# One core, decoder layer: a new deal of filler products, four banks of branch B begun early, three w_up low parts on GpSimd

## The chip, the cores and the metric

The kernel runs on 1 core of one Trainium2 chip. The metric is the device time of one execution in microseconds (us). The kernel before takes 712.83 us as the median of 3 runs (712.62 to 714.18).

## What is computed

One layer on x of 512 tokens x 1024 features, float32. Cut to what matters here:

```python
h = rms_norm(x, g_mix)
z = h @ w_in                     # q,k,v of branch A | q,k,v of branch B | gate logits
ya = swa_sink_attention(qa, ka, va, sinks, bias_a)      # window 128, 8 query heads, blocks of 128
ob = diff_attention(qb, kb, vb, lam, bias_b)            # (softmax1 - lam softmax2) V, 4 heads, causal
yb = rms_norm(ob, subln_b)
mixed = sigmoid(gA) * (ya @ w_br_a) + sigmoid(gB) * (yb @ w_br_b)
x = x + mixed @ w_o
u = causal_dwconv3(rms_norm(x, g_ffn) @ w_up)           # 1024 -> 2 x 2816
x = x + (silu(u_gate) * u_value) @ w_down
```

## The kernel before

**Products.** Every float32 factor is split into a high part (rounded by a copy) and a low part (what is left), and a product is three matmuls: high by high, high by low, low by high (`mm3`, L171 to L174). A step of 128 features against 512 tokens is three matmuls of 128x512.

**Weights.** They come in units of 128x1024, in the fixed order `worder`. `split_unit` (L125) loads a unit into `raw` on SyncE's queue, makes the high part on ScalarE (L131) and the low part on VectorE or, for the units in the set `pooled` (L158), on GpSimd (L132). `raw`, high and low have three buffers each, and `wunit` asks for one unit ahead (AHEAD = 1). So a unit's high part waits until TensorE is done with the unit three before it.

**Order of the work.** TensorE's instructions run in the order in which the code is written; those of the other engines are put in order by a scheduler when the kernel is built. Attention has many short steps that wait for VectorE and ScalarE, so between them the code calls `fill(name, i)`: it takes so many steps as the table `FILL` says out of a stream `fs` of long products that nothing waits for (gate banks, branch A's product, projections of branch B, and at the end `br_b_early`). A filler step is one `mm3`, or four for each k of a projection taken one at a time. When the stream is empty, a fill does nothing.

**Branch A (sliding window).** `fill("q")`, the heads' transposes, `fill("k")`, the key's parts (`k_parts`; high on ScalarE L463 and L465, low on VectorE L467), `fill("k2")`, and then eight units. Round i does the score of unit i (L471, L472), the transposes of unit i-1 (L626) and the product of unit i-2 (L643, L645), with the fills s1, s2, s3 behind them.

**Branch B (differential).** Sixteen units, four heads by four query blocks; unit u is head u // 4, block u % 4. Round i does:

- score i (L471, L472), then fill a[i]. Behind it on VectorE maxima (L704 where there are far keys, L706), the negative maximum (L709), on ScalarE the exponentials (L711), on VectorE the reciprocals (L714, L715), ScalarE's scaling (L716) and VectorE's difference (L717);
- the product of unit i-2 (`diff_av`: L743 with the high part, L746 with the low; then ScalarE L749, VectorE L750, ScalarE L751), then fill c;
- the transposes of unit i-1 (L727; high part on ScalarE L728, low on VectorE L729), then fill b;
- in the rounds that `r` names, a head's RMS norm (`diff_rms`: short operations on 128x4, L181 to L190 and L207, then L759 on VectorE and L761 on ScalarE) and fill d; in the rounds that `o` names, a head's transposes into yb (`diff_out`: L767; high part ScalarE L768, low VectorE L769) and fill e.

`f` are fills behind the key and query parts of heads 2 and 3; p0 to p2 stand ahead of the first unit.

**End of branch B.** Once head 2 is out, `br_b_early` joins the stream: it begins EARLY banks of yb @ w_br_b with their first three steps (heads 0 to 2). After head 3, the early banks get their fourth step, first the two matmuls that need only the high part (L878), then the third (L882); the other banks (8 - EARLY) are made in full. `mix` behind each bank (L868, L869 on VectorE; the split on ScalarE L871 and GpSimd L872) makes the left side of W_o. `late` starts two banks of W_o with steps 0 to 5 of both, then steps 6 and 7.

**w_up.** 44 banks, each with a `conv` behind it: L956 on VectorE scales by the tokens' row `rbc`, which is ready only after the fourth bank; L959 and L969 are ScalarE's, L963, L964 and L971 VectorE's. w_down follows as seven products of halves.

Of the kernel before, what the change touches and what calls it, by code (L numbers as in the profile page):

```python
# [65 lines left out]

FILL = dict(r=[5, 9, 13, 16], o=[6, 10, 14, 16], e=[5, 1, 1, 40], kv=4, up=3, warm=8, q=7, k=19, k2=4,
            s1=[0, 3, 0, 3, 2, 4, 4, 0, 0, 3], s2=[2, 3, 0, 5, 1, 7, 5, 5, 0, 0],  # L70
            s3=[3, 0, 2, 5, 6, 2, 2, 6, 0, 1], p0=4, p1=3, p2=10, ud=6, pd=[8, 9], f=[9, 0],
            a=[6, 1, 7, 8, 10, 2, 0, 5, 0, 2, 7, 3, 6, 0, 0, 5],
            b=[6, 2, 4, 4, 2, 7, 2, 1, 2, 2, 0, 0, 1, 4, 2, 2], c=[3, 0, 0, 0, 2, 0, 0, 0, 2, 1, 0, 0, 1, 0, 0, 0],
            d=[1, 0, 0, 5], v0=4)
AHEAD = 1
EARLY = 5


@with_exitstack
def tile_decoder_layer(ctx: ExitStack, tc: tile.TileContext, x4, wall, cst_d, relb_d, oneh_d, xn_d, out):  # L80
# [1091 lines left out]
```

## Time and profile before

| what | value |
|---|---|
| median of 3 runs | 712.83 us (712.62 to 714.18) |
| the profiled execution | 711.81 us |
| its span, first to last instruction | 710.0 us |
| mean granted TensorE clock | 0.995 |
| VectorE busy | 486.1 us |
| ScalarE busy | 371.3 us |
| GpSimd busy | 196.8 us |
| low parts on VectorE | 102, mean 1226 ns |
| low parts on GpSimd | 33, mean 2411 ns |

The profile is of one execution. Rows of the timeline read: start, duration, engine, line, operation, what is written and read, the tile's form, the count, and in brackets the idle time of the engine before it and who ended it. A matmul row's duration is modelled and overlaps the next; the start-to-start time of two rows is what a matmul costs. "PEld" is the load of a matmul's weights. In the rows of a table by windows stand the window, its length, then busy time and count of TensorE, weight load, VectorE, ScalarE and GpSimd, the granted clock, the share of DMA and GB/s.

### The profile page before, as it was taken

The page shows a single profiled execution, that of the slowest core. Times are in us where ns is not written, and L with a number is a line of the kernel's source. Part 1 is how long each engine was busy: PE and PEld are TensorE (multiplying, and loading weights), DVE is VectorE, ACT ScalarE, POOL GpSimd, SP SyncE. Part 2 cuts the span into 40 slices and gives each one's busy share as a digit, 9 for nine tenths or more (in the row PEclk, how much of TensorE's full clock was granted, in tenths as well). Part 3 has the DMA queues.
Part 4 walks back from the last instruction along what each step waited for, and adds up shares of the span by engine and source line. Part 5 has one row for each costly group of instructions (what it writes and reads, how often), then busy time and mean ns, then how long its engine had stood idle before and what let it go on. Part 6 is the DMA issues. An engine that isn't in the chain of part 4 may idle for free.

```text
span 710.0 us, 9146 instructions
## 1 busy us (share of the span) xinstructions
PE 690.0 (97%) x3220; PEld 568.2 (80%) x3220; DVE 486.1 (68%) x978; ACT 371.3 (52%) x690; POOL 196.8 (28%) x168
## 2 busy tenths in 40 slices
PE   7999999999999989989999999999999999999997
PEld 5897888778888867768888788888888888888886
DVE  5686786567517787585438868777767677788783
ACT  5537777865336867434325344343334334766661
POOL 2144254533347310283300514332123120100000
PEclk9999999999999999999999999999999999999999
DMA  8672112112232211035422896997986432566773
GB/s 306 260 267 90 60 60 90 59 60 90 70 109 69 80 60 61 30 108 163 144 90 79 281 297 190 324 292 196 266 237 158 138 107 87 162 192 188 228 219 107
DMA packets 28493, 107.86 MB, mean 152 GB/s; under 512 B 3652, under 2 KB 3936, under 8 KB 27936
## 3 DMA queue, kind: packets, MB, share of 16 engines
q1 hardware_dynamic: 21568, 73.67, 31.0%
q0 software_dynamic: 4816, 18.92, 11.9%
q10 hardware_dynamic: 2064, 14.70, 5.5%
q8 instruction: 25, 0.41, 0.2%
q14 instruction: 20, 0.16, 0.1%
HBM read 105.16 MB, written 29.64 MB: 190 GB/s over the span
## 4 chain that ended last, share of the span: by engine, by line
PE 87%; DVE 5%; ACT 5%; issue 1%; DMA 1%; SPq 0%; ACTq 0%; DVEq 0%
PE pj L174 22%; PE pj L172 22%; PE pj L173 22%; PE at L173 5%; PE at L174 5%; PE at L172 5%; DVE g L869 1%; PE at L472 1%; PE at L471 1%; DMA g<-in_x_dram 1%; DVE wlo L132 1%; PE at L626 1%; ACT p L711 1%; DVE g L868 1%; PE at L442 1%
## 5 line engine op out<-in xcount | busy, mean ns | idle before, releaser
L131 ACT ACTIVATE whi<-raw 128x1024 fp32r<-128x1024 f32 x135 | 139.4, 1035 | 152.7 <-PE pj L173 99.1
L172 PE MATMUL pj<-xg,whi 128*128 128x512 f32 x480 | 189.5, 395 | 0.0
L174 PE MATMUL pj<-xg,wlo 128*128 128x512 f32 x480 | 187.7, 391 | 1.2 <-DVE wlo L132 1.2
L173 PE MATMUL pj<-xg,whi 128*128 128x512 f32 x480 | 187.6, 391 | 0.0
L132 DVE TENSOR_TENSOR wlo<-raw,whi 128x1024 fp32r<-128x1024 f32 x102 | 124.8, 1226 | 35.5 <-ACT whi L131 35.0
L132 POOL TENSOR_TENSOR wlo<-raw,whi 128x1024 fp32r<-128x1024 f32 x33 | 79.4, 2411 | 113.8 <-ACT whi L131 108.2
L174 PEld LDWEIGHTS pj<-xg,wlo 128*128 128x128 f32 x480 | 90.4, 188 | 20.6 <-DVE wlo L132 1.7
L172 PEld LDWEIGHTS pj<-xg,whi 128*128 128x128 f32 x480 | 90.5, 189 | 18.1 <-ACT whi L131 0.4
L173 PEld LDWEIGHTS pj<-xg,whi 128*128 128x128 f32 x480 | 90.4, 188 | 17.9
L172 PE MATMUL pj<-whi,xg 128*128 128x512 f32 (+1 forms) x156 | 59.2, 379 | 1.8 <-ACT xg L286 1.8
L956 DVE TENSOR_TENSOR u<-pj,rbc 128x512 f32<-128x512 f32 x44 | 30.2, 689 | 42.2 <-PE pj L174 42.1
L174 PE MATMUL pj<-whi,xg 128*128 128x512 f32 (+1 forms) x156 | 58.3, 374 | 0.1
L173 PE MATMUL pj<-wlo,xg 128*128 128x512 f32 (+1 forms) x156 | 58.0, 372 | 0.0
L172 PE MATMUL at<-whi,xg 128*128 128x512 f32 x146 | 57.3, 393 | 0.0
L174 PE MATMUL at<-whi,xg 128*128 128x512 f32 x146 | 57.0, 390 | 0.0
L173 PE MATMUL at<-wlo,xg 128*128 128x512 f32 x146 | 56.9, 390 | 0.0
L959 ACT ACTIVATE yc<-u,cst 128x512 f32<-128x512 f32 x44 | 35.3, 806 | 9.4 <-DVE u L956 9.1
L963 DVE SCALAR_TENSOR_TENSOR yc<-u,cst,yc 128x511 f32<-128x511 f32 x44 | 35.6, 810 | 2.9 <-ACT yc L959 2.9
L969 ACT ACTIVATE yc<-yc 128x512 f32<-128x512 f32 x22 | 13.9, 632 | 44.6 <-DVE yc L964 44.2
L172 PEld LDWEIGHTS pj<-whi,xg 128*128 128x128 f32 x156 | 29.9, 192 | 7.0 <-ACT xg L286 2.2
L964 DVE SCALAR_TENSOR_TENSOR yc<-u,cst,yc 128x510 f32<-128x510 f32 x44 | 34.1, 777 | 1.3
L174 PEld LDWEIGHTS pj<-whi,xg 128*128 128x128 f32 x156 | 29.8, 191 | 5.7 <-DVE xg L287 0.5
(251 smaller groups left out, 1152.0 us busy)
## 6 DMA issues: line engine op xcount, KB each, us to landing
raw<-in_w_dram SPq DMA_DIRECT2D x108, 512.0 KB, 3.4
tsum<-in_w_dram POOLq DMA_DIRECT2D x24, 512.0 KB, 11.8
raw<-tsum SPq DMA_DIRECT2D x20, 512.0 KB, 3.7
tsum<-in_w_dram ACTq DMA_DIRECT2D x12, 512.0 KB, 6.9
tsum<-tsum ACTq DMA_DIRECT2D x12, 512.0 KB, 6.4
scr<-scr POOLq DMA_DIRECT2D x1, 2304.0 KB, 11.3
xnat<-in_xn_dram SPq DMA_DIRECT2D x2, 1024.0 KB, 9.4
tmp<-in_x_dram POOLq DMA_DIRECT2D x8, 256.0 KB, 3.3
```

Source lines behind the costliest of these rows:

```text
L131: nc.scalar.activation(hi[:, :width], raw[:, :width], AF.Copy)
L132: eng.tensor_tensor(lo[:, :width], raw[:, :width], hi[:, :width].bitcast(F32), ALU.subtract)
L172: nc.tensor.matmul(ps, a[0], b[0], start=start, stop=False, skip_group_check=skip)
L173: nc.tensor.matmul(ps, a[0], b[1], start=False, stop=False, skip_group_check=skip)
L174: nc.tensor.matmul(ps, a[1], b[0], start=False, stop=stop, skip_group_check=skip)
L442: nc.tensor.transpose(ps[:, t * P:(t + 1) * P], zs[t][:, c0:c0 + P], ident)
L471: nc.tensor.matmul(ps, q[:, qsl], kh[:, ksl], start=True, stop=False)
L956: nc.vector.tensor_tensor(u, ps, rbc2, ALU.mult)
L959: i = nc.scalar.activation(y, u, AF.Identity, bias=cst[:, C_CB + ch:C_CB + ch + 1], scale=cw[2])
L963: nc.vector.scalar_tensor_tensor(y[:, 1:S], u[:, 0:S - 1], cw[1], y[:, 1:S], ALU.mult, ALU.add)
L964: nc.vector.scalar_tensor_tensor(y[:, 2:S], u[:, 0:S - 2], cw[0], y[:, 2:S], ALU.mult, ALU.add)
L969: nc.scalar.activation(yg, yg, AF.Silu)
```

## The change

Three things, with no change to what is computed and none to the number of TensorE's matmuls.

1. `FILL` is dealt out anew: fewer or more filler steps at many places, head 1's output two rounds later (o from 10 to 12), head 3's norm named 17 instead of 16, which is the same round.
2. EARLY is 4 instead of 5: three filler steps fewer in the stream, and one full bank more behind head 3.
3. `pooled` also holds units 4 to 6 of w_up: their low parts move from VectorE to GpSimd.

```diff
-FILL = dict(r=[5, 9, 13, 16], o=[6, 10, 14, 16], e=[5, 1, 1, 40], kv=4, up=3, warm=8, q=7, k=19, k2=4,
-            s1=[0, 3, 0, 3, 2, 4, 4, 0, 0, 3], s2=[2, 3, 0, 5, 1, 7, 5, 5, 0, 0],
...
+FILL = dict(r=[5, 9, 13, 17], o=[6, 12, 14, 17], e=[5, 0, 2, 40], kv=4, up=3, warm=8, q=7, k=17, k2=7,
+            s1=[2, 0, 0, 3, 2, 2, 3, 0, 11, 3], s2=[0, 4, 0, 4, 1, 1, 5, 5, 2, 0],
...
-EARLY = 5
+EARLY = 4
...
-    pooled = {u + i for u, n in ((U_DA, 4), (U_VB, 4), (U_DB, 4), (U_BRA, 4), (U_GATE, 16), (U_BRB + 3, 1)) for i in range(n)}
+    pooled = {u + i for u, n in ((U_DA, 4), (U_VB, 4), (U_DB, 4), (U_BRA, 4), (U_GATE, 16), (U_BRB + 3, 1), (U_UP + 4, 3)) for i in range(n)}
```

**TensorE at score 11.** Before, head 1's output (L767) stands ahead of score 11 (L471, L472), which reads keys `qv`; `pj` is a gate bank, a filler.

```order
L172 MATMUL pj_2707<-xg_182,whi_2608 128x512
L173 MATMUL pj_2707<-xg_183,whi_2608 128x512
L174 MATMUL pj_2707<-xg_182,wlo_2609 128x512
L767 MATMUL at_2744<-ident,o_2301 128x128 x4
L172 MATMUL pj_2707<-xg_193,whi_2608 128x512
L173 MATMUL pj_2707<-xg_194,whi_2608 128x512
L174 MATMUL pj_2707<-xg_193,wlo_2609 128x512
L471 MATMUL at_2757<-qv_2466,qv_2453 128x512
L472 MATMUL at_2757<-qv_2464,qv_2453 128x512
L471 MATMUL at_2763<-qv_2467,qv_2454 128x512
L472 MATMUL at_2763<-qv_2465,qv_2454 128x512
```

Now the same gate bank ends behind score 11, and the product of unit 9 (L743) follows at once:

```order
L472 MATMUL at_2750<-qv_2456,qv_2445 128x512
L172 MATMUL pj_2707<-xg_182,whi_2608 128x512
L173 MATMUL pj_2707<-xg_183,whi_2608 128x512
L174 MATMUL pj_2707<-xg_182,wlo_2609 128x512
L172 MATMUL pj_2707<-xg_193,whi_2608 128x512
L173 MATMUL pj_2707<-xg_194,whi_2608 128x512
L174 MATMUL pj_2707<-xg_193,wlo_2609 128x512
L743 MATMUL at_2771<-vb_1834,ath_2731 128x256
L743 MATMUL at_2771<-vb_1837,ath_2731 128x256
L746 MATMUL at_2771<-vb_1834,atl_2732 128x128
L746 MATMUL at_2771<-vb_1837,atl_2732 128x128
```

Head 1's output has gone from here to behind unit 11's transposes, and unit 9's product stands three filler steps earlier behind score 11 than it did (before, three more steps of the next gate bank lay between).

**VectorE at units 14 and 15.** `p_2943` is unit 14's before, `p_3007` unit 15's. Before, unit 14's difference (L717) follows the low part of a weight of branch B and comes ahead of unit 15's maxima:

```order
L132 TENSOR_TENSOR wlo_3076<-raw_3073,whi_3075 128x1024
L717 SCALAR_TENSOR_TENSOR p_2943<-p_2943,drc_2962 128x384
L769 SCALAR_TENSOR_TENSOR y_2354<-at_2997,gsub,y_2353 128x512
L704 ISA p_3007,m_630_3013<-at_3010,cst 128x256
L704 ISA m_630_3013 128x1
L704 ISA p_3007,m_632_3019<-at_3016,cst 128x256
L704 ISA m_632_3019 128x1
L706 ISA p_3007,dmx_3008<-at_3010,bias_b,m_630_3013 128x256
L706 ISA dmx_3008 128x1
L706 ISA p_3007,dmx_3008<-at_3016,bias_b,m_632_3019 128x256
L706 ISA dmx_3008 128x1
L709 TENSOR_SCALAR dnmx_3022<-dmx_3008 128x2
```

Now unit 14's tile is `p_2961`, with `drc_2980`:

```order
L704 ISA p_3007,m_632_3019<-at_3016,cst 128x256
L704 ISA m_632_3019 128x1
L714 RECIPROCAL drc_2980<-dsm_2963 128x2
L706 ISA p_3007,dmx_3008<-at_3010,bias_b,m_630_3013 128x256
L706 ISA dmx_3008 128x1
L715 TENSOR_TENSOR drc_2980<-drc_2980,neglam 128x1
L706 ISA p_3007,dmx_3008<-at_3016,bias_b,m_632_3019 128x256
L706 ISA dmx_3008 128x1
L132 TENSOR_TENSOR wlo_3095<-raw_3092,whi_3094 128x1024
L717 SCALAR_TENSOR_TENSOR p_2961<-p_2961,drc_2980 128x384
L709 TENSOR_SCALAR dnmx_3022<-dmx_3008 128x2
```

The order of unit 14's L717 and unit 15's maxima is turned round: L769 and unit 15's four operations, and the low part, all come first, and unit 15's L709 has gone behind L717.

**VectorE in w_up.** `u_3970` is the bank c = 7 after L956, `wlo_3942` the low part for c = 8, `wlo_3993` for c = 9. Before:

```order
L956 TENSOR_TENSOR u_3970<-pj_3945,rbc_3620 128x512
L132 TENSOR_TENSOR wlo_3942<-raw_3939,whi_3941 128x1024
L963 SCALAR_TENSOR_TENSOR yc_3972<-u_3970,cst,yc_3972 128x511
L964 SCALAR_TENSOR_TENSOR yc_3972<-u_3970,cst,yc_3972 128x510
L971 TENSOR_TENSOR g_3979<-yc_3933,yc_3972 128x512
L132 TENSOR_TENSOR wlo_3993<-raw_3990,whi_3992 128x1024
L956 TENSOR_TENSOR u_4021<-pj_3996,rbc_3620 128x512
```

Now:

```order
L956 TENSOR_TENSOR u_3970<-pj_3945,rbc_3620 128x512
L963 SCALAR_TENSOR_TENSOR yc_3972<-u_3970,cst,yc_3972 128x511
L964 SCALAR_TENSOR_TENSOR yc_3972<-u_3970,cst,yc_3972 128x510
L971 TENSOR_TENSOR g_3979<-yc_3933,yc_3972 128x512
L956 TENSOR_TENSOR u_4021<-pj_3996,rbc_3620 128x512
L132 TENSOR_TENSOR wlo_3993<-raw_3990,whi_3992 128x1024
L132 TENSOR_TENSOR wlo_4032<-raw_4029,whi_4031 128x1024
```

The low part for c = 8 now stands two banks earlier (behind the L956 of c = 5), and that for c = 9 has gone behind the L956 of c = 8.

More of the change, by code (lines that the diff above doesn't have):

```diff
@@ L65 @@
 F_ORDER = [f + NH * j for f in range(NH) for j in range(2)]
-FILL = dict(r=[5, 9, 13, 16], o=[6, 10, 14, 16], e=[5, 1, 1, 40], kv=4, up=3, warm=8, q=7, k=19, k2=4,
-            s1=[0, 3, 0, 3, 2, 4, 4, 0, 0, 3], s2=[2, 3, 0, 5, 1, 7, 5, 5, 0, 0],
[L71 to L74, printed above, removed]
+FILL = dict(r=[5, 9, 13, 17], o=[6, 12, 14, 17], e=[5, 0, 2, 40], kv=4, up=3, warm=8, q=7, k=17, k2=7,
+            s1=[2, 0, 0, 3, 2, 2, 3, 0, 11, 3], s2=[0, 4, 0, 4, 1, 1, 5, 5, 2, 0],
+            s3=[5, 1, 2, 4, 8, 3, 6, 6, 0, 1], p0=4, p1=1, p2=10, ud=6, pd=[8, 9], f=[11, 0],
+            a=[6, 1, 6, 8, 10, 2, 0, 4, 1, 1, 7, 2, 6, 0, 4, 5],
+            b=[6, 0, 5, 6, 4, 7, 0, 1, 2, 1, 0, 1, 3, 5, 1, 1], c=[6, 0, 0, 0, 2, 0, 0, 0, 2, 1, 0, 3, 3, 0, 0, 0],
+            d=[0, 1, 4, 5], v0=4)
 AHEAD = 1
-EARLY = 5
+EARLY = 4
 @with_exitstack
```

## The prediction

> **What bounds the kernel now.** I read the busy shares first, then the chain that ended last, then the list of waits, and at last the timeline around every wait.
>
> ```profile
> PE 690.0 (97%) x3220; PEld 568.2 (80%) x3220; DVE 486.1 (68%) x978; ACT 371.3 (52%) x690; POOL 196.8 (28%) x168
> PE 87%; DVE 5%; ACT 5%; issue 1%; DMA 1%; SPq 0%; ACTq 0%; DVEq 0%
> PE at L767 <- ACT o L761: 4.2, 3, 2.5
> PE pj L174 <- DVE wlo L132: 2.3, 2, 1.2
> PE pj L173 <- POOL qv L872: 1.5, 2, 0.7
> PE at L727 <- DVE p L717: 1.3, 1, 1.3
> PE at L472 <- DVE qv L467: 0.8, 1, 0.8
> ```
>
> TensorE is the bound, and the change leaves its matmuls as they are in number and size. So the time can only move by what TensorE waits, and by its clock. The waits shown here are some 10 us of 710; those in places that the new table leaves alone (the 1.3 us of L727 belong to the first differential unit) stay. What is quoted below as a wait is taken from start to start of two matmuls less the ordinary step, because a wait also costs about 0.1 us of restart. The ordinary step is read off in the rows below: 0.23 us for 128x512 (273.19 to 273.41), 0.11 to 0.12 for the small ones (the first L767 row, about 0.1 each), so a filler product of three matmuls is 0.68 us.
>
> **First SWA score.** Before, L472 waits for the low half of the query (L467).
>
> ```profile
> 66.50 0.22 PE L471 MATMUL at<-qv,qv 128*128 128x128 f32 x1
> 67.54 0.33 PE L472 MATMUL at<-qv,qv 128*128 128x128 f32 x1 [0.82 <-DVE qv L467]
> ```
>
> 1.04 us from start to start less 0.11 is 0.93. The table gives three products more ahead of it (k2 from 4 to 7), 3 x 0.68 = 2.04 us against 0.93: the wait goes. The next transposes lose one product of cover (k from 19 to 17), which has room for most of it; I allow 0 to +0.3. Term: -0.9.
>
> **Output of head 1 (dOUT(1), L767).** Its wait begins on GpSimd.
>
> ```profile
> 250.53 2.40 POOL L132 TENSOR_TENSOR wlo<-raw,whi 128x1024 fp32r<-128x1024 f32 x1 [5.07 <-ACT whi L131]
> 250.84 2.11 DVE L186 TENSOR_TENSOR t<-t,tv 128x4 f32<-128x4 f32 x1
> 255.32 0.68 ACT L761 ACTIVATE o<-o,y 128x128 f32<-128x128 f32 x2
> 255.76 0.62 PE L767 MATMUL at<-ident,o 128*128 128x128 f32 x3 [2.46 <-ACT o L761]
> 256.58 0.37 ACT L728 ACTIVATE ath<-at 128x256 fp32r<-128x256 f32 x1
> 250.00:262.00 12.00, 9.54 (x41) 7.40 (x40) 10.26 (x36) 6.39 (x17) 2.40 (x1) 0.86 0.14 45
> 262.00:282.00 20.00, 18.36 (x97) 14.74 (x97) 16.66 (x67) 14.47 (x43) 0.00 (x0) 1.00 0.25 79
> ```
>
> A 128x4 operation takes 2.11 us while GpSimd makes a low part; its neighbours take 0.16. Everything behind it on VectorE and ScalarE is 2 us late, and TensorE stands 2.46 us. Then the granted clock is 0.86 over these 12 us and 1.00 after them: 12 x 0.14 = 1.7 us, of which I count 1.5 as lost work. The place costs 2.6 + 1.5 = 4.1 us. The Trainium skill, "SBUF — State Buffer", section "SBUF: two separate sides", says that a VectorE operation with two SBUF inputs and a GpSimd operation that reads SBUF lock each other out for a whole instruction; the 2.11 us agree.
>
> The change sets the output two units later, but not the queues that feed it: ScalarE still does L761, L761, L716, L749 and then L728, and unit 9's product (L743) needs that L728. On the clock of before TensorE reaches this L743 at about 254.7: it came to dOUT(1) at 255.76 - 2.63 = 253.13, and instead of that output it now does one filler product (0.68) and score 11 (4 x 0.23). The high part is there at 256.95: it waits 2.3, and some 0.5 more for the low part made behind it. That is 2.8 for 2.6, and about as good a chance (three in four) of the 1.5 of clock: 2.8 + 1.2 = 4.0. Term: -0.1, from -2.5 (VectorE isn't locked out this time) to +0.3.
>
> The Trainium skill, "TensorE: Matmul & The Clock Gate", Part 1, sets the clock back only after an idle window of some 3.4 us; here 2.46 us were followed by 0.86, so the trace doesn't bear the rule out as a bound on one gap. By the rule no gap here would cost clock; that is a rival below.
>
> **Units 13 and 14.** Four waits in 9 us:
>
> ```profile
> 269.59 0.74 PE L743 MATMUL at<-vb,ath 128*128 128x256 f32 x4 [0.22 <-ACT ath L728]
> 272.35 0.34 PE L743 MATMUL at<-vb,ath 128*128 128x256 f32 x1
> 272.74 0.33 PE L746 MATMUL at<-vb,atl 128*128 128x128 f32 x1
> 273.19 0.39 PE L173 MATMUL pj<-xg,whi 128*128 128x512 f32 x1
> 273.41 0.40 PE L174 MATMUL pj<-xg,wlo 128*128 128x512 f32 x1
> 273.92 0.41 PE L727 MATMUL at<-ident,p 128*128 128x128 f32 x2
> 276.69 0.39 PE L174 MATMUL pj<-xg,wlo 128*128 128x512 f32 x1
> 278.34 0.73 PE L767 MATMUL at<-ident,o 128*128 128x128 f32 x4 [1.26 <-ACT o L761]
> ```
>
> 0.22; 0.39 - 0.12 = 0.27 at L746; 0.51 - 0.23 = 0.28 at L727; 1.65 - 0.23 = 1.42 at L767 (head 2): 2.2. In the new order head 1's output and more filler stand ahead of each, by 1 to 4 us of work, and all four go. Term: -2.2.
>
> **The end of branch B.** This is paid for with the last units' cover. There is one bank less to begin early, so three filler products (2.04 us) stand behind the last head instead of among units 14 to 16, and VectorE's order is worse: the low part of a weight (L132) and the next score's four operations now come ahead of unit 14's L717. Its rows:
>
> ```profile
> 278.03 1.23 DVE L132 TENSOR_TENSOR wlo<-raw,whi 128x1024 fp32r<-128x1024 f32 x1
> 279.83 0.75 DVE L769 SCALAR_TENSOR_TENSOR y<-at,gsub,y 128x512 fp32r<-128x512 f32 x1
> 282.31 0.72 ACT L711 ACTIVATE p<-p,dnmx 128x512 f32<-128x512 f32 x1 [2.00 <-DVE dnmx L709]
> 283.65 0.19 ACT L711 ACTIVATION_READ_ACCUMULATOR p<-p,dnmx 128x1 f32 x1
> 285.38 0.75 DVE L717 SCALAR_TENSOR_TENSOR p<-p,drc 128x512 f32<-128x512 f32 x1
> 286.93 0.60 ACT L728 ACTIVATE ath<-at 128x512 fp32r<-128x512 f32 x1 [0.42 <-PE at L727]
> 293.10 0.73 PE L767 MATMUL at<-ident,o 128*128 128x128 f32 x4 [0.46 <-ACT o L761]
> 293.87 0.69 ACT L768 ACTIVATE y<-at,gsub 128x512 fp32r<-128x512 f32 x1 [0.53 <-PE at L767]
> 294.61 0.50 PE L878 MATMUL pj<-y,whi 128*128 128x512 f32 x1
> ```
>
> I count from the start of score 14 on TensorE as 0. VectorE is done with head 2's scaling at 0.5, then does L500 (0.65), score 14's four (1.7), L750, L709 and L729 (0.7) and L769 (0.7), to 4.3; score 15's four with unit 14's L714 and L715 among them (2.0), to 6.3; L132 (1.1), to 7.4; and then L717 for three key blocks (0.6), to 8.0. TensorE by then has done two scores (0.7 + 0.9), unit 12's product and unit 13's transposes (0.45), head 2's (0.45), five filler products (3.4 + 0.3 of waiting, below) and unit 13's product (0.45), to 6.6. So unit 14's transposes wait 1.45. ScalarE can begin score 15's two L711 only after L717 and L709, at 8.2; they take 1.5 (282.31 to 283.84), then L751 and L728 to 10.5, while TensorE is at 9.1: the product of unit 14 waits 1.65 with its low part. Unit 15's L717 ends at 11.95, TensorE is at 11.5: 0.5. With one filler product for cover, its product waits 0.4. Five filler products (3.4 us) stand ahead of head 3's output as now, so its 0.62 stays. L878 now follows head 3's transposes at once: 294.61 - 293.54 (the end of four of 0.11) = 1.07, less 0.11 or so, 0.94. The third filler product behind head 2 may wait for L769, 0 to 1.1; I take 0.3. Sum: 1.45 + 1.65 + 0.5 + 0.4 + 0.62 + 0.94 + 0.3 = 5.9. Before has here 0.24 at unit 15's transposes, 0.62, and 0.37 at L878: 1.2. Term: +4.6, from 0 (the queues run in another rhythm than my walk's) to +5.8.
>
> **Mix and W_o.** With four full banks instead of three ahead of W_o, GpSimd's L872 has 2.7 us more lead.
>
> ```profile
> 309.95 0.50 PE L173 MATMUL pj<-qv,whi 128*128 128x512 f32 x1 [0.72 <-POOL qv L872]
> 311.64 0.50 PE L173 MATMUL pj<-qv,whi 128*128 128x512 f32 x1 [0.73 <-POOL qv L872]
> 312.90 0.50 PE L173 MATMUL pj<-act,whi 128*128 128x512 f32 x1 [0.30 <-POOL act L872]
> 315.19 0.50 PE L174 MATMUL pj<-qv,wlo 128*128 128x512 f32 x1 [1.10 <-DVE wlo L132]
> ```
>
> These are 0.72 + 0.73 + 0.30 + 1.10 = 2.85 of idle and with the restarts (0.16 each) 3.5; 0.3 more is the low part of branch B's last weight, which one more bank also covers. The W_o weight's low part moves ahead of the last two mix steps on VectorE, so its 1.27 goes, and those two steps come up to 1.2 later: I leave 1.2 standing. Term: 1.2 - 3.8 = -2.6, from -3.8 to -1.5.
>
> **w_up.** Three low parts of 1.23 on VectorE become three of 2.40 on GpSimd. TensorE waits once in this stage:
>
> ```profile
> 400.10 0.69 DVE L956 TENSOR_TENSOR u<-pj,rbc 128x512 f32<-128x512 f32 x1 [0.40 <-PE pj L174]
> 401.98 0.50 PE L174 MATMUL pj<-xg,wlo 128*128 128x512 f32 x1 [1.23 <-DVE wlo L132]
> ```
>
> The low part stands behind L956 of the bank before it. VectorE gains 3.7 us, and the scheduler turns this into putting this low part earlier and the next one behind its L956: same cover (two matmuls, 0.45), same wait, one bank on. Term: 0; -1.4 if the gained time does dissolve it, +1.2 if a GpSimd low part locks VectorE out of the short operations (L215, L220) that make the row scale rbc ahead of it: they would start 2.40 - 1.23 = 1.2 later. There the end of that chain has room, since VectorE itself stands 2.07 us for TensorE:
>
> ```profile
> 378.33 0.69 DVE L1013 COPY rbc<-at 128x512 f32<-128x512 f32 x1 [2.07 <-PE at L221]
> ```
>
> **Sum.** -0.9 - 0.1 - 2.2 + 4.6 - 2.6 + 0 = -1.2 us. On the profiled execution (711.81 us, of which 710.0 are the span) that makes 710.6; the median of the runs shown, 712.83, lies 1.0 above it, and less 1.2 is 711.6. The runs shown spread 1.5 us, about one loss of clock; so 0.2% (1.43 us) is what can be told from no change.
>
> **The rivals.**
>
> *The waits at the end don't form, or by half.* The walk chains VectorE's and ScalarE's queues over 12 us, and an earlier start of one of them by 1 us takes 1 us from each of two waits. For it: TensorE's other waits of before, of 2.2 us, go, and so it comes to the end later against its helpers. Against it: L717 behind L132 is in the order itself. Half the term is -2.3: 709.3; the whole, 707.0.
>
> *The end costs clock (slower).* Between unit 14's transposes and unit 15's product TensorE would stand some 4 us in 8, more than the 2.46 that were followed by 0.86. One loss is +1.5 (713.1); a clock that stays down over both waits costs +3.0, 714.6. It decides when the two waits of unit 14 lie at 1.5 each with under 1 us of work between them.
>
> *No gap costs clock.* If the 0.86 came from something else than the wait, unit 9's wait is without its 1.2: 710.4.
>
> *GpSimd's low parts lock VectorE out in w_up*: +1.2, 712.8, and with one more wait behind it 714.
>
> **How the numbers follow.** The forecast, with its terms within 1.5 us of their sum (710.1 to 713.1): 0.40. The end without its waits, or half: 0.25. The end with loss of clock: 0.20. No loss at unit 9: 0.10. GpSimd in w_up: 0.05. Faster than 711.4: 0.15 of the forecast's 0.40, 0.22 of the second, 0.08 of the fourth, 0.45. Slower than 714.26: 0.14 of the third, 0.03 of the last and 0.04 of the forecast's edge, 0.21. The rest, 0.34, is no change. The range takes half of the second case and the third up to both waits: 708.2 to 715.0.
>
> **What would show it.** Right: no wait at L472's first score and at the output of heads 1 and 2; L743 of unit 9 waits 2 to 3 us, with a clock under 0.9 behind it; L727 of unit 14 waits over 1 us for L717; L878 waits about 0.9 for L768; at most one wait for L872 over 0.5; one wait for L132 in w_up, of about 1.2. The prediction is wrong in its main term if units 14 and 15 wait under 1 us together, and in its cover if L743 of unit 9 doesn't wait.

## The result and the profile after

The changed kernel takes 706.79 us as the median of 5 runs (705.03 to 708.57). The ratio to the kernel before, run beside it, is 0.9923, with a 95% interval of 0.9901 to 0.9945, or some 5.5 us less. The forecast was 1.2 us less, and 708.2 was the low end of its range: the direction was right and the size wrong. The profiled execution took 705.03 us, with a span of 703.3 and a granted clock of 1.00. It is the fastest of the five; the others show clocks of 0.993 to 0.998 and times up to 708.57.

The busy shares and the head of TensorE's list of waits, after (total, times, longest):

```profile
PE 686.9 (98%) x3220; PEld 567.1 (81%) x3220; DVE 484.5 (69%) x975; ACT 370.9 (53%) x690; POOL 204.6 (29%) x171
PE at L743 <- ACT ath L728: 2.6, 2, 1.6
PE at L727 <- DVE p L717: 1.7, 2, 1.3
PE pj L174 <- DVE wlo L132: 1.5, 1, 1.5
PE pj L173 <- POOL act L872: 1.2, 1, 1.2
PE at L727 <- DVE dnmx L709: 0.8, 1, 0.8
PE pj L878 <- ACT y L768: 0.8, 1, 0.8
PE at L767 <- ACT o L761: 0.5, 1, 0.5
```

The 4.2 us at head outputs are down to 0.5, L472's 0.8 is gone, and the three waits for the mix have become one. L743's wait for L728 has grown from 0.2 to 2.6; L727 for L709 and L878 for L768 are new. Three low parts have gone from VectorE to GpSimd (975 instructions for 978, 171 for 168).

**Where the time went.** The list leaves out restarts and slow matmuls. So for every trace I took the start of each matmul less the start of the one before it, less the ordinary step (0.227 us for 128x512, 0.109 to 0.176 for the smaller), and added this up by place. "Start" is the first 16 us, "sliding" 60 to 100 us, "first unit" 100 to 160 us (the first differential units), "middle" from unit 9 to head 2's output, "end" from there to the last matmul of the early banks (L882). The ratios are those of the timed runs, the lost time that of one profiled execution. Rows below "after" are the experiments.

| kernel | start | sliding | first unit | middle | end | mix, W_o | w_up | sum | ratio, 95% |
|---|---|---|---|---|---|---|---|---|---|
| before | 4.9 | 2.6 | 3.5 | 7.55 | 1.45 | 4.6 | 1.7 | 27.2 | 1 |
| after | 3.6 | 0.9 | 3.5 | 2.8 | 5.3 | 1.7 | 1.8 | 20.4 | 0.9923 (0.9901-0.9945) |
| e1_swa | 3.3 | 0.9 | 3.6 | 7.4 | 1.45 | 4.6 | 1.7 | 23.6 | 0.9978 (0.9967-0.9989) |
| e2_early | 3.6 | 2.6 | 3.5 | 7.3 | 5.0 | 1.35 | 1.8 | 26.0 | 1.0008 (0.9996-1.0019) |
| e3_pool | 3.3 | 2.6 | 3.4 | 7.3 | 1.5 | 4.6 | 1.75 | 25.3 | 1.0000 (0.9991-1.0010) |
| e4_diff | 3.5 | 2.6 | 3.5 | 2.8 | 4.3 | 4.6 | 1.7 | 23.8 | 0.9984 (0.9967-1.0001) |
| e9_early5 | 2.9 | 0.9 | 3.55 | 2.8 | 4.85 | 4.6 | 1.7 | 22.1 | 0.9955 (0.9942-0.9968) |
| h1_out1 | 3.3 | 2.6 | 3.4 | 5.9 | 2.5 | 4.6 | 1.8 | 25.1 | 0.9988 (0.9978-0.9997) |
| e5_late15 | 5.1 | 2.6 | 3.5 | 7.8 | 1.4 | 4.6 | 1.8 | 27.7 | 1.0011 (1.0002-1.0019) |
| e6_late15 | 3.5 | 0.9 | 3.55 | 2.4 | 6.4 | 1.7 | 1.8 | 21.0 | 0.9922 (0.9908-0.9936) |
| e10_q15 | 3.3 | 0.9 | 3.6 | 2.1 | 5.9 | 1.7 | 1.8 | 20.1 | 0.9922 (0.9908-0.9935) |
| e11_all2 | 3.4 | 0.9 | 2.4 | 2.4 | 6.4 | 1.5 | 1.8 | 19.7 | 0.9913 (0.9901-0.9926) |
| e7_brb2 | 4.95 | 0.9 | 3.5 | 2.8 | 5.1 | 1.7 | 1.75 | 21.5 | 0.9941 (0.9929-0.9954) |
| e8_up9 | 3.6 | 0.9 | 3.5 | 4.1 | 6.4 | 1.7 | 8.2 | 29.2 | 1.0033 (1.0020-1.0045) |
| h3_half_brb2 | 3.8 | 0.9 | 2.45 | 2.4 | 4.05 | 1.5 | 1.7 | 17.7 | 0.9877 (0.9862-0.9892) |
| h4_all4 | 4.9 | 1.1 | 2.7 | 2.0 | 6.2 | 2.1 | 1.7 | 21.5 | 0.9902 (0.9885-0.9918) |
| h2_after | 3.5 | 0.9 | 3.6 | 2.8 | 5.4 | 1.7 | 1.7 | 20.4 | 0.9932 (0.9914-0.9951) |

The last row is the changed kernel once more. "Start" moves between 2.9 and 5.1 without regard to the edit and is no part of the change: in the four kernels with 4.9 or more (before, e5_late15, e7_brb2, h4_all4) a wait of 1.7 to 2.2 us for ScalarE's L286 is followed by a granted clock of 0.72 over 10 to 16 us, and in the others that clock is 1.00. Without it the change is worth -1.7 in the sliding window, -4.75 in the middle, +3.85 at the end and -2.9 at the mix: -5.5, which is what the runs give. That the two agree so closely is in part luck, since the profiled execution is the fastest of the changed kernel's five.

**The middle.** After, from the timeline (start, duration, engine, operation, idle before):

```profile
246.94 2.40 POOL L132 TENSOR_TENSOR wlo<-raw,whi 128x1024 fp32r<-128x1024 f32 x1 [5.08 <-ACT whi L131]
247.25 2.11 DVE L186 TENSOR_TENSOR t<-t,tv 128x4 f32<-128x4 f32 x1
253.41 0.50 PE L743 MATMUL at<-vb,ath 128*128 128x256 f32 x2 [1.57 <-ACT ath L728]
254.16 0.44 PE L746 MATMUL at<-vb,atl 128*128 128x128 f32 x2 [0.25 <-DVE atl L729]
248.00:260.00 12.00, 10.18 (x50) 8.10 (x49) 10.06 (x39) 8.57 (x26) 1.34 (x1) 1.00 0.26 81
260.00:270.00 10.00, 9.99 (x58) 8.52 (x58) 8.65 (x35) 6.94 (x23) 0.00 (x0) 1.00 0.19 63
```

VectorE is held for 2.11 us as before, and TensorE pays at unit 9's L743 instead of at head 1's output. But it pays 2.2 (with the low part, start to start), no clock is lost, and in the next window it is busy for 9.99 of 10 us.

**The end.** After, from the timeline:

```profile
274.90 1.22 DVE L132 TENSOR_TENSOR wlo<-raw,whi 128x1024 fp32r<-128x1024 f32 x1
276.04 0.61 DVE L717 SCALAR_TENSOR_TENSOR p<-p,drc 128x384 f32<-128x384 f32 x1
276.77 0.72 ACT L711 ACTIVATE p<-p,dnmx 128x512 f32<-128x512 f32 x1 [0.45 <-DVE dnmx L709]
276.80 0.52 PE L727 MATMUL at<-ident,p 128*128 128x128 f32 x3 [0.79 <-DVE dnmx L709]
279.00 0.62 PE L743 MATMUL at<-vb,ath 128*128 128x256 f32 x3 [0.99 <-ACT ath L728]
280.50 0.63 PE L727 MATMUL at<-ident,p 128*128 128x128 f32 x4 [0.35 <-DVE p L717]
287.15 0.73 PE L767 MATMUL at<-ident,o 128*128 128x128 f32 x4 [0.47 <-ACT o L761]
288.66 0.50 PE L878 MATMUL pj<-y,whi 128*128 128x512 f32 x1 [0.78 <-ACT y L768]
```

This is the forecast's chain, link by link: the low part, L717 right behind it, then L711, and TensorE late at unit 14's transposes and product, at unit 15's, at head 3's output and at L878. The release that the row of 276.80 names is L709, which ends at 276.73; the L717 that its transposes read ends 0.08 us before, at 276.65.

### The profile page after: what moved, and what is told of

The parts are those of the page before. It is cut to its first block, busy times and chain, and to the rows that moved or that the text cites. A ratio compares the mean times of both kernels' runs of the same rounds, so it can differ in the third digit from the quotient of the medians.

```text
span 703.3 us, 9142 instructions
## 1 busy us (share of the span) xinstructions
PE 686.9 (98%) x3220; PEld 567.1 (81%) x3220; DVE 484.5 (69%) x975; ACT 370.9 (53%) x690; POOL 204.6 (29%) x171
## 4 chain that ended last, share of the span: by engine, by line
PE 86%; DVE 5%; ACT 5%; DMA 2%; issue 1%; POOL 1%; SPq 0%; ACTq 0%
PE pj L174 22%; PE pj L172 22%; PE pj L173 22%; PE at L174 5%; PE at L173 5%; PE at L172 5%; DMA g<-in_x_dram 1%; PE at L472 1%; ACT p L711 1%; PE at L471 1%; PE at L626 1%; PE at L442 1%; DMA tsum<-in_w_dram 1%; DVE wlo L132 1%; ACT whi L131 1%
## 5 line engine op out<-in xcount | busy, mean ns | idle before, releaser
L172 PE MATMUL pj<-xg,whi 128*128 128x512 f32 x480 | 188.8, 393 | 0.0
L174 PE MATMUL pj<-xg,wlo 128*128 128x512 f32 x480 | 187.2, 390 | 1.5 <-DVE wlo L132 1.5
L132 DVE TENSOR_TENSOR wlo<-raw,whi 128x1024 fp32r<-128x1024 f32 (+1 forms) x99 | 121.7, 1231 | 34.8 <-ACT whi L131 34.2
L132 POOL TENSOR_TENSOR wlo<-raw,whi 128x1024 fp32r<-128x1024 f32 x36 | 86.8, 2415 | 131.8 <-ACT whi L131 123.6
L174 PEld LDWEIGHTS pj<-xg,wlo 128*128 128x128 f32 x480 | 90.1, 188 | 20.9 <-DVE wlo L132 1.9
L172 PEld LDWEIGHTS pj<-xg,whi 128*128 128x128 f32 x480 | 90.2, 188 | 17.8
L956 DVE TENSOR_TENSOR u<-pj,rbc 128x512 f32<-128x512 f32 x44 | 30.2, 690 | 47.4 <-PE pj L174 47.3
L172 PE MATMUL pj<-whi,xg 128*128 128x512 f32 (+1 forms) x156 | 58.4, 374 | 0.9 <-ACT xg L286 0.9
L174 PE MATMUL pj<-whi,xg 128*128 128x512 f32 (+1 forms) x156 | 57.6, 369 | 0.1
L172 PE MATMUL at<-whi,xg 128*128 128x512 f32 x146 | 57.3, 392 | 0.0
L174 PE MATMUL at<-whi,xg 128*128 128x512 f32 x146 | 56.9, 390 | 0.0
L964 DVE SCALAR_TENSOR_TENSOR yc<-u,cst,yc 128x510 f32<-128x510 f32 x44 | 33.6, 765 | 1.3
L172 PEld LDWEIGHTS pj<-whi,xg 128*128 128x128 f32 x156 | 29.5, 189 | 6.0 <-ACT xg L286 1.3
L174 PEld LDWEIGHTS pj<-whi,xg 128*128 128x128 f32 x156 | 29.4, 189 | 5.5 <-DVE xg L287 0.5
```

The costliest lines, as they stand in the source:

```text
L132: eng.tensor_tensor(lo[:, :width], raw[:, :width], hi[:, :width].bitcast(F32), ALU.subtract)
L172: nc.tensor.matmul(ps, a[0], b[0], start=start, stop=False, skip_group_check=skip)
L174: nc.tensor.matmul(ps, a[1], b[0], start=False, stop=stop, skip_group_check=skip)
L956: nc.vector.tensor_tensor(u, ps, rbc2, ALU.mult)
L964: nc.vector.scalar_tensor_tensor(y[:, 2:S], u[:, 0:S - 2], cw[0], y[:, 2:S], ALU.mult, ALU.add)
```

## The experiments

My theory after the result: the 2 us by which VectorE and ScalarE come late are one debt, paid once by TensorE at whatever reads them next. Clock that is lost after the wait does not come on top of it, because a slow TensorE is waited for less by what follows; and the new deal of filler hides the rest. The rivals were that the parts are independent and one of them had simply been priced wrong, that the gain is mostly that of not losing clock, and that GpSimd's lock could be moved out of the way altogether.

### Each part by itself

e1_swa is the kernel before with the sliding window's new numbers.

```diff
-k=19, k2=4, s1=[0, 3, 0, 3, 2, 4, 4, 0, 0, 3], ...
+k=17, k2=7, s1=[2, 0, 0, 3, 2, 2, 3, 0, 11, 3], ...   (new s2 and s3 too)
```

> The kernel before with only the sliding window part of the new table (k, k2, s1, s2, s3). Theory of cover (the traces' waits add up, place by place): the first score's wait of 0.93 goes and the waits at the first transposes fall from 1.1 to 0.4, so -1.0 to -1.7 us against before, and the outputs of branch B wait as before. Rival (the gain is mostly fewer losses of clock, which strike anywhere): nothing from the waits; the time moves only as far as the run's mean clock does, 0.8 to 1.7 us for each 0.0024 of it.

Measured: 709.2 us, 0.9978; only the column "sliding" differs from before by more than chance, by 1.7. The timed gain is 1.6 us.

e2_early is the kernel before with four early banks.

```diff
-EARLY = 5
+EARLY = 4
```

> The kernel before with only EARLY = 4. Theory of cover: mix and W_o wait 1.5 instead of 4.4 us (-2.9), head 3's output loses two products of cover (+1.4) and L878 its one (+0.6): -0.9 us in sum. Rival (lead in front of W_o is worth little, GpSimd's steps are the bound there): the wait for L872 stays at 2 us or more, and the time is +1 to +2.

Measured: 711.73 us, 1.0008, no difference that can be told. The mix gives 3.25 and the end takes 3.55. From its timeline:

```profile
291.55 0.73 PE L767 MATMUL at<-ident,o 128*128 128x128 f32 x4 [1.83 <-ACT o L761]
294.23 0.63 PE L878 MATMUL pj<-y,whi 128*128 128x512 f32 x1
294.66 0.63 PE L878 MATMUL pj<-y,wlo 128*128 128x512 f32 x1
```

Head 3's output now waits 1.83 instead of 0.46, and behind it the matmuls are 0.43 apart instead of 0.23: the bank that was taken away had been head 3's cover. Some 1.6 of the 3.55 is this slow clock (0.83 over 290 to 300 us). It may be usual here: eleven of the twelve executions show a clock of 0.996 or less, and the one at 1.00 took 708.87 us.

e3_pool is the kernel before with the three low parts of w_up on GpSimd.

```diff
-... (U_BRB + 3, 1))
+... (U_BRB + 3, 1), (U_UP + 4, 3))
```

> The kernel before with only the three w_up low parts on GpSimd. Theory of cover: the one wait of 1.4 us in w_up moves one bank on and stays between 1.2 and 1.7: -0.1 to +0.3 us. Rival (VectorE's relief is what made the kernel faster): the wait falls under 0.5, and the time by 1 us or more.

Measured: 710.81 us, 1.0000; w_up loses 1.75 instead of 1.7. By itself this part is worth nothing either way.

e4_diff is the kernel before with the differential branch's new numbers (r, o, e, p1, f, a, b, c, d), five early banks and the old sliding window.

> The kernel before with only branch B's part of the new table (r, o, e, p1, f, a, b, c, d), five banks early. Theory of cover: head 1's wait becomes unit 9's (2.2 instead of 2.6), units 13 and 14 lose 2.4, the end gains 3.0 (L878 still covered), so -0.4 + -2.4 + 3.0 = +0.2 without the clock, and -1.3 where the clock isn't lost behind unit 9. Rival (the new deal itself is the gain): -3 us or more, with an end that waits less than 2 us in all.

Measured: 709.66 us, 0.9984. The middle falls from 7.55 to 2.8 and the end grows from 1.45 to 4.3.

The four parts add up to -1.6 + 0.6 + 0.0 - 1.1 = -2.1 us, and the whole is -5.5. Each is known to about 1 us, so a pair of them belongs together.

e9_early5 is the changed kernel with EARLY = 5.

> The changed kernel with EARLY = 5 again. Cover theory: L878's wait of 0.9 is covered by the fifth bank's three products (-0.7), mix and W_o wait 4.4 instead of 1.5 (+2.9): 2.2 us slower than the changed kernel, that is 3 us faster than before. So EARLY = 4 would be worth 2.2 with the new deal and nothing with the old one (e2_early). Rival (the parts add up: EARLY = 4 is worth as little here as alone): within 0.7 us of the changed kernel.

Measured: 707.99 us, 0.9955, against 0.9923. Under the new deal four banks are worth 0.0032 x 711 = 2.3 us (1.6 by h2_after's 0.9932), under the old one nothing that can be told. At the end the new deal leaves its waits standing with or without a fifth bank: with it 4.3 in e4_diff and 4.85 here, where this execution lost clock at the end and e4_diff did not, without it 5.3. So the bank costs some 1 us there, and given to the mix it brings 2.9 (4.6 to 1.7). The two edits of FILL and EARLY can't be judged apart.

### The lock in the middle

h1_out1 is the kernel before with head 1's output alone two rounds later.

```diff
-o=[6, 10, 14, 16]
+o=[6, 12, 14, 16]
```

> The kernel before with only head 1's output two rounds later (o from 10 to 12; its one filler step moves with it), nothing else dealt anew. Lag theory (VectorE's and ScalarE's queues are some 2 us late from the locked L186 on, and TensorE pays this at whatever comes first, until filler is put there): TensorE passes score 11 and then waits at unit 9's product (1.3 in all) and more than before at unit 11's product; all waits and lost clock between unit 9 and head 2 stay near 7 us, against 7.4 before and 2.5 in the changed kernel: 0 to -1 us. Rival (the place of head 1's output is what gave the gain): they fall to 4.5 or less, -2.5 us or more.

Measured: 710.2 us, 0.9988. The 2.46 us at head 1's output are gone and unit 9's product waits only 0.78, but unit 11's, later in the same stretch, waits 1.68 and unit 12's 1.10:

```profile
255.42 0.51 PE L743 MATMUL at<-vb,ath 128*128 128x256 f32 x2 [0.78 <-ACT ath L728]
266.60 0.62 PE L743 MATMUL at<-vb,ath 128*128 128x256 f32 x3 [1.68 <-ACT ath L728]
270.62 0.38 PE L743 MATMUL at<-vb,ath 128*128 128x256 f32 x1 [1.10 <-ACT ath L728]
```

The middle loses 5.9, which lies between the two theories (7 and 4.5 or less), and the end 1.05 more than before: 1.65 of the 4.75 come from moving the output, the other 3.1 with the rest of branch B's new numbers, which no run here takes apart. The time, 0.9 us less, fits the lag theory.

e5_late15 is the kernel before with GpSimd's low part of the last gate weight held back until head 1's norm is through; e6_late15 is the same in the changed kernel. A GpSimd copy of eight columns, overwritten at once by the low part, makes it wait; the orders of the other engines stay as they were.

```diff
+        i == U_GATE + 15 and eng.tensor_copy(lo[:, 0:8], OS[1][0][:, 3 * P:3 * P + 8])
         eng.tensor_tensor(lo[:, :width], raw[:, :width], hi[:, :width].bitcast(F32), ALU.subtract)
...
-        o, ss = dpo[h]
+        o, ss = OS[h] = dpo[h]
```

> The kernel before, with one GpSimd low part (the last gate weight's) held back until head 1's norm is scaled: GpSimd first copies 8 columns of the scaled head into the low tile. No other engine's order changes. Lock theory (the 2.1 us in which VectorE stands are what delays head 1's output): L186 takes 0.16, head 1's wait falls from 2.6 to about 0.6, no clock is lost there, and the waits of units 11 to 14 (2.2 us with the clock lost, 3.7 without) stay: 1.5 to 2 us faster than before. Rival (the queues are behind anyway): the wait moves on to unit 11's product in full, no change within 0.7 us.

> The changed kernel with the same GpSimd low part held back until head 1's norm is scaled. Lock theory: unit 9's wait (1.74 + 0.1 + 0.4 = 2.2 us) falls to 0.3 or less and nothing new waits, so -2.0 us against the changed kernel (some 704.8 where that takes 706.8; a ratio to before near 0.9895). Rival: the wait reappears at unit 10 or 11, and the time is that of the changed kernel.

Measured: 711.69 us, 1.0011, and 705.75 us, 0.9922 (the changed kernel 0.9923). In the timeline of the first:

```profile
251.05 0.16 DVE L186 TENSOR_TENSOR t<-t,tv 128x4 f32<-128x4 f32 x1
254.21 2.39 POOL L132 TENSOR_TENSOR wlo<-raw,whi 128x1024 fp32r<-128x1024 f32 x1
254.81 2.21 DVE L717 SCALAR_TENSOR_TENSOR p<-p,drc 128x384 f32<-128x384 f32 x1 [0.75 <-ACT p L716]
268.70 0.50 PE L743 MATMUL at<-vb,ath 128*128 128x256 f32 x2 [2.00 <-ACT ath L728]
```

L186 takes 0.16 us again, and head 1's output waits 0.68 instead of 2.63. But now the low part falls on an L717, which takes 2.21 instead of 0.61, and the wait comes back further on, 2.00 at unit 11's product. The debt has moved, and the middle loses 7.8, some 1.6 of it clock lost behind that wait. In the second, unit 9's L743 no longer waits, L746 waits 1.72 instead for an L729 that comes late behind an L717 held for 2.21, and the kernel's time is the same. Both were expected to gain 1.5 us or more. Moving the long instruction gained nothing in either kernel: another operation that TensorE needs stood beside it.

e10_q15 is the changed kernel with that low part in four pieces, e11_all2 with all of GpSimd's low parts in two.

```diff
-        eng.tensor_tensor(lo[:, :width], raw[:, :width], hi[:, :width].bitcast(F32), ALU.subtract)
+        [eng.tensor_tensor(lo[:, c], raw[:, c], hi[:, c].bitcast(F32), ALU.subtract)
+         for c in cuts(width, 4 if i == U_GATE + 15 else 1)]    # e11_all2: 2 if i in pooled
```

> The changed kernel with the last gate weight's GpSimd low part cut into four instructions of 256 columns, every engine's order else as it is. Theory (what costs is the length for which one GpSimd instruction shuts VectorE out, so short ones let VectorE through in between): L186 takes under 0.9 instead of 2.1 us, unit 9's wait falls from 2.2 to about 1, -1.0 to -1.5 us against the changed kernel. Rival (four short locks cost as much as a long one): unit 9 waits 1.9 or more, no change.

> The changed kernel with all 36 GpSimd low parts cut into two instructions of 512 columns. Theory of short locks: half of unit 9's wait (-1.1) and 0 to -0.7 elsewhere, so -1.1 to -1.8 us against the changed kernel. Rival (a GpSimd instruction has a fixed cost, so 36 more of them make the low parts late): new waits for L132 of GpSimd, +0.5 us or more.

Measured: 704.73 us, 0.9922, and 704.3 us, 0.9913. In the timeline of e10_q15, then in e11_all2's groups (busy, mean ns) and timeline, and the same operation in the kernel before:

```profile
246.99 0.46 DVE L186 TENSOR_TENSOR t<-t,tv 128x4 f32<-128x4 f32 x1
```

```profile
L132 POOL TENSOR_TENSOR wlo<-raw,whi 128x512 fp32r<-128x512 f32 x72 | 92.4, 1304 | 127.4 <-ACT whi L131 114.5 <-issue 8.0 <-PE pj L174 4.9
144.68 0.41 DVE L709 TENSOR_SCALAR dnmx<-dmx 128x2 f32<-128x2 f32 x1
```

```profile
147.83 1.51 DVE L709 TENSOR_SCALAR dnmx<-dmx 128x2 f32<-128x2 f32 x1
```

VectorE gets in between two pieces. L186 takes 0.46 instead of 2.11 and unit 9's L743 waits 1.09 instead of 1.74; with halves everywhere a wait at the first differential unit falls from 1.46 to 0.38. The middle gains 0.7 and the first unit 1.1. Both executions lost clock at the end, which gives much of it back there (5.9 and 6.4 for 5.3). The ratios of e10_q15 and of the changed kernel can't be told apart, where 1.0 to 1.5 us less was expected; e11_all2's interval overlaps it too. So shorter waits are shown here, and a shorter time is not.

### Wait and clock

g1_gaps is the changed kernel with five high parts of w_up repeated (`REP = {12: 8, 18: 9, 24: 10, 30: 11, 36: 12}`), which lays gaps into a stretch that is otherwise without any. The matmuls of L174 stand at its L176, those of L172 at its L174.

> The changed kernel with the high part of five w_up weights (banks 12, 18, 24, 30, 36) made 8 to 12 times over on ScalarE, so that TensorE waits for them by different lengths in an otherwise even stretch. If the clock goes by a single idle gap's length with an edge near 2 us: every gap over 2.4 us is followed by some 3.4 us of half-rate matmuls (0.43 instead of 0.23 apart) and none under 1.7. If it goes by chance (where the gap falls in some window): gaps of like length are sometimes followed by them and sometimes not. If by an edge of 3.4 us: only the gaps above that.

Measured in a single execution: 751.45 us, span 749.7, clock 0.972. Its list of waits, the window behind the first gap (its last figures are the clock, the DMA share and GB/s), and two matmuls in it:

```profile
PE pj L174 <- ACT whi L133: 30.7, 5, 7.9
426.00:432.00 6.00, 5.77 (x14) 4.09 (x15) 5.52 (x4) 0.36 (x2) 5.92 (x6) 0.55 0.51 152
428.47 0.63 PE L175 MATMUL pj<-xg,whi 128*128 128x512 f32 x1
428.89 0.63 PE L176 MATMUL pj<-xg,wlo 128*128 128x512 f32 x1
```

All five gaps (7.89, 5.55, 3.68, 7.73 and 5.86 us) are followed by matmuls 0.43 us or more apart, for 3 to 7 us. Here the clock is a cost of its own, since nothing waits behind it. That it was none in the middle of the kernel before is shown by runs that didn't lose it. In e3_pool the same 2.46 us stand at head 1's output, and the clock of the 12 us around it is 1.00:

```profile
254.12 0.73 PE L767 MATMUL at<-ident,o 128*128 128x128 f32 x4 [2.46 <-ACT o L761]
248.00:260.00 12.00, 9.54 (x50) 7.62 (x49) 10.26 (x37) 6.40 (x16) 2.40 (x1) 1.00 0.13 45
267.22 0.74 PE L743 MATMUL at<-vb,ath 128*128 128x256 f32 x4 [1.12 <-ACT ath L728]
268.46 0.66 PE L746 MATMUL at<-vb,atl 128*128 128x128 f32 x4 [0.50 <-DVE atl L729]
```

Yet the middle loses 7.3 there and 7.55 in the kernel before. Unit 11's product, which waited 0.38 and 0.15 behind the slow matmuls of before, waits 1.28 and 0.66 here (start to start): 1.41 us more, about the price of the lost clock. e2_early, which keeps the clock there, and e1_swa, which loses it, come to the same total too (7.3 and 7.4).

In the changed kernel it is otherwise, since its filler leaves no such wait behind unit 9. In e8_up9 (below), whose waits at unit 9 are those of the changed kernel, the clock is 0.86 over 248 to 260 us, and the middle loses 4.1 instead of 2.8: there the lost clock comes on top. So the theory holds only where a wait stands behind.

### Other low parts, and a better kernel

e7_brb2 is the changed kernel with the low part that stands ahead of unit 14's L717 on GpSimd too.

```diff
-(U_BRB + 3, 1)
+(U_BRB + 2, 2)
```

> The changed kernel with the low part of branch B's third weight on GpSimd too: L132 no longer stands ahead of unit 14's L717. Queue theory (the end waits because of what stands ahead of L717 on VectorE): unit 14's transposes wait 0.0 to 0.2 instead of 0.96, unit 14's product and unit 15's some 1.0 less together, so -1.5 to -2 us against the changed kernel. Rival (GpSimd's 2.4 us lock VectorE out at the same place, longer than the 1.2 of the low part): the waits of the end stay at 4.5 us or more, 0 to +1 us.

Measured: 706.23 us, 0.9941. Unit 14's transposes wait 0.32 instead of 0.96 and its product 0.20 instead of 1.16. But a filler product waits 0.83 for L769, unit 15's transposes wait 0.9, and the end loses 5.1 instead of 5.3: an L709 ahead of that L769 takes 1.59 us beside the new GpSimd low part, so a lock took the place of the long instruction.

e8_up9 is the changed kernel with one more low part of w_up on GpSimd, the one that TensorE waits for.

```diff
+(U_UP + 9, 1)
```

> The changed kernel with the low part for w_up's bank 9 on GpSimd too. Queue theory (the one wait of w_up is the low part that stands behind L956 of the bank before): the wait of 1.6 us is gone, -1.6 us against the changed kernel. Rival (it moves one bank on once more, as it did from 8 to 9): a wait of 1 us or more at bank 10, same time.

Measured: 712.78 us, 1.0033. From its list of waits and its timeline:

```profile
PE pj L174 <- POOL wlo L132: 5.9, 1, 5.9
402.50 2.58 POOL L142 DMA_DIRECT2D tsum<-in_w_dram  x3
404.20 3.24 POOL L132 TENSOR_TENSOR wlo<-raw,whi 128x1024 fp32r<-128x1024 f32 x1
403.51 4.49 DVE L964 SCALAR_TENSOR_TENSOR yc<-u,cst,yc 128x510 f32<-128x510 f32 x1
```

On GpSimd the low part stands behind three accumulating DMA issues and begins at 404.20; an L964 that VectorE begins during the issues takes 4.49 us instead of 0.77. A wait of 1.47 has become one of 5.94 with a loss of clock behind it.

h3_half_brb2 is e11_all2 with e7_brb2's edit; h4_all4 is the changed kernel with all of GpSimd's low parts in quarters; h2_after is the changed kernel again, on the same chip.

> The changed kernel with all GpSimd low parts in two instructions and branch B's third weight's low part on GpSimd as well. Theory of short locks: what the end won in e7_brb2 (L717 not behind L132) is no longer given back to the lock, so the end waits some 1.5 us less than the 5 of the changed kernel, on top of what the halves gave (1.1 at the first differential unit, 0.4 at unit 9): -2 to -3 us against the changed kernel. Rival: the end is bound by the chain of softmax steps, not by the low part, and waits 4.5 or more: the time of e11_all2, 0.6 to 1 us below the changed kernel.

> The changed kernel with all GpSimd low parts in four instructions of 256 columns. If the lock's length is all that counts: unit 9's wait near 1.4 and the first differential unit's near 0.4, -1.8 to -2.2 us against the changed kernel. If the added time of each instruction counts (0.74 us for a quarter against 1.30 for a half and 2.42 for a whole, so 0.54 us more for a weight than whole): the low parts come later and waits for L132 of GpSimd appear; no better than the halves, -0.5 or worse.

> The changed kernel once more, to stand beside the three others on one chip. All theories: 5 to 6 us faster than before.

Measured: 702.49 us, 0.9877 (0.9862 to 0.9892); 703.76 us, 0.9902 (0.9885 to 0.9918); 705.92 us, 0.9932 (0.9914 to 0.9951). h3_half_brb2 beats both kernels, the changed one by 0.0046 to 0.0055 of 711 us, some 3 to 4 us. Two rows of its list of waits, and its timeline at the end:

```profile
PE at L743 <- ACT ath L728: 1.2, 1, 1.2
PE at L727 <- DVE p L717: 0.9, 2, 0.7
273.82 0.17 DVE L709 TENSOR_SCALAR dnmx<-dmx 128x2 f32<-128x2 f32 x1
274.13 0.62 DVE L717 SCALAR_TENSOR_TENSOR p<-p,drc 128x384 f32<-128x384 f32 x1
278.01 0.63 PE L727 MATMUL at<-ident,p 128*128 128x128 f32 x4 [0.73 <-DVE p L717]
```

With the low part of 1.22 us off VectorE and GpSimd's locks halved, L717 follows L709 at once and unit 14 hardly waits (0.25 at its transposes, 0.20 at its product); 4.05 is left of the end's 5.3. Each edit alone gave less than its share (e11_all2 0.9913, e7_brb2 0.9941): one leaves the long instruction on VectorE, the other puts it on GpSimd as a lock. Quarters by themselves (h4_all4) can't be told from halves by themselves (e11_all2); cutting costs GpSimd time (a whole low part 2.42 us, four of 0.74 make 2.96), and the profiled execution of h4_all4 lost clock at the end.

## Why the prediction was wrong

**First sliding score: right, too small.** Forecast -0.9, measured -1.7 (e1_swa alone: -1.6 us). The wait at L472 went as said. The rest I had not looked for, so it is luck: the transposes of the third unit, the first with two key blocks, waited 1.08 and now wait 0.42. VectorE's L602, a 128x4 operation, took 0.94 us beside a GpSimd low part that runs from 78.67 to 81.08; now no low part runs beside it. Counted from the first score, the unit's exponentials on ScalarE start 1.2 us earlier and TensorE comes 0.4 earlier. Before and after:

```profile
80.17 0.94 DVE L602 SCALAR_TENSOR_TENSOR nmx<-mx,negsink 128x4 f32<-128x4 f32 x1
81.14 0.51 ACT L607 ACTIVATE s<-s,nmx 128x256 f32<-128x256 f32 x1 [0.99 <-DVE nmx L602]
```

```profile
79.14 0.15 DVE L602 SCALAR_TENSOR_TENSOR nmx<-mx,negsink 128x4 f32<-128x4 f32 x1
79.33 0.51 ACT L607 ACTIVATE s<-s,nmx 128x256 f32<-128x256 f32 x1 [0.21 <-DVE nmx L602]
```

**Output of head 1: the step that failed.** The forecast was "2.8 for 2.6, and about as good a chance (three in four) of the 1.5 of clock: 2.8 + 1.2 = 4.0", a term of -0.1. With the next term the middle was to gain 2.3, and it gained 4.75. Of the 2.45 that I missed, 1.2 is the clock that the term charges again at unit 9 and that the run didn't lose; 0.6 is unit 9's wait, 2.2 instead of 2.8, since TensorE reached that product 4.4 us behind L186's start and not 3.9; and the rest, some 0.65, was lost in before and not counted. Of that, 0.31 is at unit 11's product, which from start to start waits 0.38 and 0.15 where the sum has only the idle 0.22; the remainder is small steps.

The mistake behind these sizes is that the prediction priced the 2 us, the clock and the later waits as independent costs. e1_swa, e2_early and e3_pool show that they are not: they lose 7.3 to 7.4 with the clock lost or kept. In e3_pool, which kept it, the waits behind head 1's output are 1.94 at unit 11's product, 0.27, 0.27 and 1.42, or 3.9 where the next term has 2.2; in before, the slow matmuls had hidden 1.41 of them. The new filler took away all 3.9. e5_late15 shows the same debt at other places.

The mechanism at unit 9 was right: the wait did form, for L728, with 2.11 us of lock ahead of it. The clock under 0.9 that I had expected behind it didn't come, in this trace or in h2_after's. Of the seven traces with this wait (after, h2_after, e4_diff, e7_brb2, e8_up9, e9_early5, g1_gaps) only e8_up9 shows it, at 1.3 us: the price was about right and the chance of three in four too high. How often it strikes in the timed executions stays open. The rival that no gap costs clock is refuted all the same (g1_gaps).

**Units 13 and 14: right, too small.** The four waits are gone. They were 2.5 us in that trace, counted from start to start, and 3.9 in one that kept the clock.

**End of branch B: right, a little too large.** Forecast +4.6, measured +3.85. Unit 14's transposes waited 0.96 for 1.45 and its product 1.39 for 1.65, unit 15's 0.52 and 0.41 for 0.5 and 0.4, head 3's output 0.63 for 0.62, L878 0.94 for 0.94 (and 0.11 in its row), and the filler product behind head 2 nothing for 0.3. The sum is 4.96 for 5.9. The walk had L717 done 8.0 us behind the start of score 14 and TensorE there at 6.6; in the trace it is 7.1 and 6.3. The rival that the waits don't form is refuted. The rival of a loss of clock there didn't come true in the profiled run; it is real in e6_late15, e8_up9, e9_early5, e10_q15, e11_all2 and h4_all4 (0.88 over 276 to 290 us), and may be part of why the changed kernel's runs spread from 705.03 to 708.57 while their clocks go from 1.00 to 0.993.

**Mix and W_o: right.** -2.9 for -2.6. One wait is left, 1.42 and 0.11 behind it, where 1.2 was forecast:

```profile
307.47 0.50 PE L173 MATMUL pj<-act,whi 128*128 128x512 f32 x1 [1.25 <-POOL act L872]
```

**w_up: right.** One wait for L132 of 1.47 and its restart, at 400.61, and e3_pool at 1.0000.

Put together: -0.8 at the first score, -2.45 in the middle, -0.7 at the end and -0.3 at the mix make the -4.3 between forecast and measurement. More than half of it is the middle, where I priced single waits and a loss of clock one by one and did not ask what a delay of 2 us becomes when the first wait for it is taken away.

## What to carry to other kernels

When a helper engine falls behind by some microseconds, count that delay once, follow it to where the filler behind it ends, and charge lost clock only if no wait stands behind that would have taken up the same time. Judge a table of filler and the amount of filler together: four banks instead of five gained nothing that can be told under one deal and some 2 us under another. A long GpSimd instruction beside short VectorE operations is worth cutting in pieces: here that shortened the waits, while moving it only moved them. The time fell clearly only when a low part left VectorE as well (h3_half_brb2). Look up first what is queued on GpSimd ahead of an instruction that you move there.

## What the runs showed of the hardware

- **The clock after a gap does not follow from its length alone.** Of the gaps in the traces, those of 3.68 us and more were followed by half-rate matmuls in 6 of 6 cases (five in g1_gaps, one in e8_up9). Those of 1.7 to 2.5 us were in 9 of 13: the same 2.46 us cost clock in before and e1_swa and not in e2_early and e3_pool. Those of 1.4 to 1.6 us were once in 22. A few waits of 1.2 us or less close together, as at the end of branch B, did in six kernels, and about the same waits didn't in after, h2_after, e4_diff and g1_gaps. The Trainium skill, "TensorE: Matmul & The Clock Gate", Part 1, sets the clock back after an idle window of some 3.4 us: the six gaps above it agree, the nine below it don't.
- **What decided in these traces is how a gap falls into fixed windows.** The granted clock of each trace changes only on a grid of 3.41 us: in before it is full for 71 such windows, half for one (256.63 to 260.05) and full for 132. On this grid 22 of the 3,655 windows at full clock, in all 18 traces, are followed by half clock, and they are the 22 with the least matmul work in them: 1.23 us or less of 3.41, where each matmul counts with its ordinary step in proportion to its columns (0.227 us for 512). The 2.46 us of before lie in one window (253.22 to 256.63), those of e3_pool across two. The lowest window without a loss is 1.23 us too, so the edge is known only as about 1.2, a bit over a third.
- **The lock falls on many of VectorE's operations, not on all.** Not only L186: an L709 of 128x2 took 1.51 us instead of 0.17, an L717 2.21 instead of 0.61. In the traces of before and after, L709 was over 0.2 us longer than its median in 17 of the 19 times that it began beside a GpSimd low part, and L630, L750 and L500, which read one factor from TensorE's output tiles, in none of 48. A low part takes GpSimd 2.42 us whole, 1.30 in halves and 0.74 in quarters, and the held operation is released between the pieces (L186 0.46).
